# Attention of a hybrid encoder layer: keys loaded for 512 queries, two live bias tables, memory weights transposed on TensorE, queries swapped at another tile, charge 0.84

## The chip, the cores and the metric

The kernel runs on one core of a Trainium2 chip. The metric is the time of one execution on the device in microseconds (us), the median of three runs: 3072.31 us before the change (3069.44 to 3073.78). Five engines work side by side, each in its own order: PE (matmul; PEld is its weight load), DVE (vector), ACT (scalar), POOL (GpSimd), and SP, which here issues every DMA. Each stands until the semaphores of its next instruction are set; what is behind that instruction on the same engine stands too.

## The reference

One layer of an encoder, applied to two sequences, 4096 and 1024 rows of 1024. A projection `w_in` makes the inputs of a Hyena branch (a long convolution), of dilated attention, of attention to 256 memory tokens, and gates; the three branches times their gates go through `w_out`. The change is in the two attentions:

```python
for window, dil in ((128, 1), (512, 4), (2048, 16)):      # 6 heads of 64
    R = window // (2 * dil)                               # always 64 keys to each side
    logits = q @ k.T * E ** -0.5 + bias[bucket((kj - qi) * dil)]   # per residue class of dil
    m = max(logits); p = exp(logits - m); s = sum(p)
    outs.append(p @ v / s); lses.append(m + log(s))
y_att = sum(softmax(lses) * outs)
y_mem = softmax(qm @ km.T * E ** -0.5) @ vm               # 4 heads, 256 tokens
```

## The kernel before

Everything is float32 in value; products take float16 pairs, high and low part, in up to three passes. Stages follow each other: the Hyena projection with the filter beside it; the q, k, v projection with the long convolution beside it; the gate projection with attention beside it (about 1640 to 2576 us); the output.

`weave` mixes two generators: each yields a charge, and the one with the smaller sum goes on. Attention's charges are multiplied by `K_A` = 0.88 while gates run (L140, L1628). This, and `ORDER`, in which a tile's scores, exps, turns and values alternate, set PE's order, which is kept word for word. The other engines and SP are ordered by a scheduler: by the priority at which the code is reached, and by when a model has operands and buffers ready; it can take a later instruction first.

`att_tiles` cuts each residue class of each dilation into groups of up to 256 queries (two tiles of 128). `work_list` mixes these, the second sequence's, and memory groups: 84 groups, 160 tiles, 40 of them memory tiles. For a group, `load_group` issues the transposing loads of the queries `qT` and of the keys `kT` (up to 384 rows: 64 more to each side), and of the values `v`. It is called when the first tile of the group two before is reached (`AHEAD` = 2), and it ends with two DVE copies that put the halves of `qT` in each other's place (`qS`, two buffers, L967 to L971): a score is the product of `qT` and `kT` plus that of `qS` and `kT`.

A tile goes through four steps, each a tile or more behind the last. Scores: PE writes `s`, DVE scales, adds the bias table `tab` and takes the maximum `mx` (L1051). Exps: ACT (L1063). After the first two heads (`XT` = 2), `crossbar` splits these into `hl` on POOL (L1079, L1080), and SP transposes `hl` into `hx` by a DMA (L1082). Turns: the other heads in pairs, four transposes on PE into `tt` (L1094), high part `th` on ACT, low part `tl` on DVE. Values: PE multiplies with `v`, or with `vm` for the memory. `attended` copies the result and the negative maximum into `y`, POOL the maximum (L1155), ACT the rest (L1156), and stores it (`yc`, `ym`). A memory tile has four heads: two by `hx`, two by `tt`. Three bias tables are loaded before the first tile.

Of the kernel before, what the change touches and what calls it, by code (L numbers as in the profile page):

```python
# [12 lines left out]
F32 = mybir.dt.float32  # L13
F32R = mybir.dt.float32r
F16 = mybir.dt.float16
I32 = mybir.dt.int32
AF = mybir.ActivationFunctionType
ALU = mybir.AluOpType
# [4 lines left out]
P = 128  # L23
# [3 lines left out]
H = 6  # L27
# [5 lines left out]
CONFIGS = ((128, 1), (512, 4), (2048, 16))  # L33
C_Q, C_MQ, C_K = 0, 768, 1280
ROW = C_K + 768
# [3 lines left out]
YW = VH + H  # L39
# [97 lines left out]

IDLE_F, K_F, C_FFN = 50000, 2.4, 2000
K_C, IDLE_1, IDLE_2, IDLE_3, IDLE_M = 1.35, (34000, 28000), (9000, 16000), 18000, 40000
K_A, IDLE_A, GATE_IDLE = 0.88, 20000, 0  # L140
LAG_I, WS_BUFS = 6, 6
MT, BATCH0 = 4, 2
MIX, K_Q = 0.1, 1.2
AHEAD = 2
XT, VLAG = 2, 4
ORDER = "etevsteeesvvsetesvsetse"
GP = 6000000
# [31 lines left out]
class Layer:  # L179
# [726 lines left out]
    def att_tiles(self):  # L906

        out = []
        for i, (off, L) in enumerate(self.seqs):
            for cf, (win, dil) in enumerate(CONFIGS):  # L910
                n = L // dil
                if n == 64:
                    for r in range(0, dil, 2):
                        out.append(dict(seq=i, cf=cf, dil=dil, r=r, n=n, pair=True, q0=0, nq=128, k0=0, k1=128))
                    continue
                assert n % 128 == 0
                for r in range(dil):
                    for q0 in range(0, n, 256):
                        q1 = min(n, q0 + 256)
                        out.append(dict(  # L920
                            seq=i, cf=cf, dil=dil, r=r, n=n, pair=False, q0=q0, nq=q1 - q0,
                            k0=max(0, q0 - 64), k1=min(n, q1 + 64),
                        ))
        return out

    def load_group(self, pool, g):
        i, nc = g["seq"], self.nc
        dil, r = g.get("dil", 1), g.get("r", 0)
        rows = self.rows[i].rearrange("(n d) c -> d n c", d=dil)
        vr = self.vrows[i].rearrange("(n d) c -> d n c", d=dil)  # L930
        qT = g["qT"] = pool.tile([P, 6, 256], F16, tag="qT", name="qT", bufs=AHEAD + 1)
        if "mem" in g:
            nc.sync.dma_start_transpose(out=qT[:, 0:4], in_=self.rows[i][g["q0"]:g["q0"] + 256, C_MQ:C_K])
            return
        kT = pool.tile([P, 6, 384], F16, tag="kT", name="kT", bufs=AHEAD + 1)
        nk = g["k1"] - g["k0"]
        v = pool.tile([P, 3, VW], F16, tag="v", name="v", bufs=2)
        if g["pair"]:
            for a in range(2):
                nc.sync.dma_start_transpose(out=kT[:, :, 64 * a:64 * a + 64], in_=rows[r + a, :, C_K:ROW])  # L940
                nc.sync.dma_start_transpose(out=qT[:, :, 64 * a:64 * a + 64], in_=rows[r + a, :, C_Q:C_MQ])
                self.ld(v[64 * a:64 * a + 64, 0, :], vr[r + a])
            g["chunks"] = {0: 0}
        else:
            nc.sync.dma_start_transpose(out=kT[:, :, :nk], in_=rows[r, g["k0"]:g["k1"], C_K:ROW])
            nc.sync.dma_start_transpose(
                out=qT[:, :, :g["nq"]], in_=rows[r, g["q0"]:g["q0"] + g["nq"], C_Q:C_MQ]
            )
            cuts = [g["k0"]] + list(range(g["q0"] + 64, g["k1"], 128))
            ends = cuts[1:] + [g["k1"]]  # L950
            g["chunks"] = {s: j for j, s in enumerate(cuts)}
            full = [j for j, (s, e) in enumerate(zip(cuts, ends)) if e - s == 128]
            part = [j for j, (s, e) in enumerate(zip(cuts, ends)) if e - s != 128]
            if full:
                f0, nf = full[0], len(full)
                assert full == list(range(f0, f0 + nf))
                self.ld(
                    v[:, f0:f0 + nf, :],
                    vr[r, cuts[f0]:cuts[f0] + 128 * nf].rearrange("(j p) c -> p j c", p=P),
                )  # L960
            for j in part:
                k = ends[j] - cuts[j]
                p0 = P - k if j else 0
                nc.gpsimd.memset(v[P - k:P, j, :] if p0 == 0 else v[0:p0, j, :], 0.0)
                self.ld(v[p0:p0 + k, j, :], vr[r, cuts[j]:ends[j]])
        g["kT"], g["v"] = kT, v
        qS = g["qS"] = pool.tile([P, 6, 256], F16, tag="qS", name="qS", bufs=2)  # L967
        for a in range(2):
            nc.vector.tensor_copy(  # L969
                qS[64 * a:64 * a + 64, :, :g["nq"]], qT[64 - 64 * a:P - 64 * a, :, :g["nq"]]  # L970
            )  # L971
# [18 lines left out]
    def attention(self, pool, ps):  # L990
        nc = self.nc
        zero = pool.tile([P, 1], F32, name="zero", bufs=1)
        nc.vector.memset(zero, 0.0)
        groups = self.work_list()
        while groups[0]["seq"] not in self.done:
            yield 500
        self.load_group(pool, groups[0])
        self.load_tables(pool)
        for g in groups[1:AHEAD]:
            self.load_group(pool, g)  # L1000
        yield IDLE_A
        tiles = [(gi, t) for gi, g in enumerate(groups) for t in range(g["nq"] // P)]
        state = {}

        def scores(n):
            gi, t = tiles[n]
            g = groups[gi]
            if t == 0 and gi + AHEAD < len(groups):
                self.load_group(pool, groups[gi + AHEAD])
            mem = "mem" in g  # L1010
            i, q0 = g["seq"], g["q0"] + t * P
            st = state[n] = dict(g=g, q0=q0, mem=mem, H=HM if mem else H)
            if mem:
                W, ls = NMEM, self.lsc[:, 1, 0:1]
                st["chunks"] = [(0, 0), (P, 1)]
                st["v"], st["lo"] = self.vm[i], HM * E1
                units = ((0, 1), (2, 3))
            else:
                ls = self.lsc[:, 0, 0:1]
                if g["pair"]:  # L1020
                    ks, ke, tb, t0 = 0, 128, self.tabp, 0
                    st["chunks"] = [(0, 0)]
                else:
                    ks, ke = max(0, q0 - 64), min(g["n"], q0 + 192)
                    tb, t0 = self.tab[g["cf"]], ks - (q0 - 64)
                    st["chunks"] = [(0, g["chunks"][ks]), (ke - ks - P, g["chunks"][q0 + 64])]
                W, kc = ke - ks, ks - g["k0"]
                st["v"], st["lo"] = g["v"], VH
                units = ((0, 2), (1, 3), (4,), (5,))
            st["W"] = W  # L1030
# [26 lines left out]
        def exps(n):  # L1057
            st = state[n]
            nh, pt, W = st["H"], st["pt"], st["W"]
            nm = st["nm"] = pool.tile([P, H], F32, tag="nm", name="nm", bufs=VLAG + 1)  # L1060
            nc.vector.tensor_scalar_mul(nm[:, :nh], st["mx"][:, :nh], -1.0)  # L1061
            for h in range(nh):
                nc.scalar.activation(out=pt[:, h, :W], in_=pt[:, h, :W], func=AF.Exp, bias=nm[:, h:h + 1])  # L1063
                if h + 1 == XT:
                    crossbar(st)
                yield 0

# [18 lines left out]
        def turns(n):  # L1086
            st = state[n]
            pt, chunks = st["pt"], st["chunks"]
            st["p"] = []
            for pr in range(XT // 2, st["H"] // 2):  # L1090
                tt = ps.tile([P, 2, 2, P], F32, tag="e", name="tt", bufs=2)
                for ci, (w0, vj) in enumerate(chunks):
                    for a in range(2):
                        nc.tensor.transpose(tt[:, a, ci, :], pt[:, 2 * pr + a, w0:w0 + P], self.ident)  # L1094
                th = pool.tile([P, 2, 2, P], F16, tag="th", name="th", bufs=4)
                tl = pool.tile([P, 2, 2, P], F16, tag="tl", name="tl", bufs=4)
                n = len(chunks)
                nc.scalar.activation(out=th[:, :, :n], in_=tt[:, :, :n], func=AF.Copy)  # L1098
                nc.vector.tensor_tensor(out=tl[:, :, :n], in0=tt[:, :, :n], in1=th[:, :, :n], op=ALU.subtract)  # L1099
# [3 lines left out]
        def values(n):  # L1103
# [1 line left out]
            chunks, v, lo = st["chunks"], st["v"], st["lo"]  # L1105
            last = len(chunks) - 1
            yp = ps.tile([P, 512], F32, tag="gf"[n % 2], name="yp", bufs=(1, 3)[n % 2])
            heads = list(range(XT, st["H"])) + list(range(XT))
            st["p"] += [(st["hx"][:, 0, h], st["hx"][:, 1, h]) for h in range(XT)]
            for pr in range(st["H"] // 2):  # L1110
                for a in range(2):
                    h = heads[2 * pr + a]
# [26 lines left out]
    def attended(self, pool, st, yp):  # L1139

        nc = self.nc
        g, q0 = st["g"], st["q0"]
        y = pool.tile([P, YW], F32, tag="y", name="y", bufs=2)
        if st["mem"]:
            sm = pool.tile([P, HM], F32, tag="sm", name="sm", bufs=3)
            yv = yp[:, :HM * E1].rearrange("p (h e) -> p h e", e=E1)
# [413 lines left out]
            t0 = b * B + t * P  # L1560
            self.st(self.out[i][t0:t0 + P, :], xr)

    def load_tables(self, pool):
        nc = self.nc
        self.tab = []
        for cf in range(3):
            t = pool.tile([P, H, 256], F32, name=f"tab{cf}", bufs=1)
            src = self.tab_d[cf]
            self.ld(t, bass.AP(src.tensor, src.offset + P - 1, [[H * 384 - 1, P], [384, H], [1, 256]]))
            self.tab.append(t)  # L1570
        bm = pool.tile([P, P], F32, tag="pt", name="bm", bufs=3)
        self.ld(bm, self.x["bmask"])
        self.tabp = pool.tile([P, H, P], F32, name="tabp", bufs=1)
        nc.gpsimd.tensor_tensor(
            out=self.tabp, in0=self.tab[2][:, :, 64:192], in1=bm.unsqueeze(1).to_broadcast([P, H, P]), op=ALU.add
        )

    def pool(self, name, space=None, side=None):
        kw = {"space": space} if space is not None else {}
# [101 lines left out]
```

## Time and profile before

| | |
|---|---|
| median of three runs | 3072.31 us (3069.44 to 3073.78) |
| the profiled execution | 3067.02 us, its span 3065.2 us |
| PE, DVE, ACT, POOL busy | 91%, 67%, 54%, 41% of the span |
| gate products | 1638.8 to 2574.6 us (first to last start) |
| value products of attention | 1574.4 to 2527.9 us |
| output products | 2576.2 to 3060.5 us |

"Busy" is the share in which the engine has an instruction at work; matmuls overlap, so that the time between two starts, not the length of one, is what PE pays. A wait is put down to what ended it. [...] Times in the rows are us from the span's start, means are ns.

### The profile page before, as it was taken

To read this page: it belongs to the slowest core of one execution; us is meant where nothing else is said; L and a number is where in the kernel's file an instruction comes from. 1 tells how busy PE (TensorE), PEld (TensorE's weight loads), DVE (VectorE), ACT (ScalarE), POOL (GpSimd) and SP (SyncE) were. 2 spreads that over 40 slices of the span, in tenths; PEclk is the share of its full clock that TensorE was granted. 3 is DMA by queue.
4 is the path that set the end of the run, shared out by engine and by line. 5 is a ranking of instruction groups with operands and counts; after the bars stand their busy time and mean duration, and the time that the engine had idled before them with its cause. 6 is when DMAs were issued, how large, how long until landed. Compare 5 with 4: busy or idle time off the path is not lost. (4 is left out here: it accounts for less than half of the span.)

```text
span 3065.2 us, 55390 instructions
## 1 busy us (share of the span) xinstructions
PE 2775.0 (91%) x19620; PEld 1725.3 (56%) x19620; DVE 2052.3 (67%) x5237; ACT 1663.4 (54%) x3149; POOL 1259.7 (41%) x1534
## 2 busy tenths in 40 slices
PE   5998989888959998999999998989899899999999
PEld 2444444333625544544456666666666665778787
DVE  7777888787648882364567666767677665665663
ACT  5666666334738884464366565656566554232321
POOL 2336777232126661142133233333344344555551
PEclk9999999999979999999999999999999999999999
DMA  7554444555559969697499999999998989777762
GB/s 224 175 151 151 155 148 146 155 164 190 208 167 230 246 200 209 214 202 176 110 222 265 216 202 203 225 210 191 210 219 197 202 172 315 250 239 252 236 223 97
DMA packets 761855, 610.38 MB, mean 199 GB/s; under 512 B 514958, under 2 KB 702262, under 8 KB 758122
## 3 DMA queue, kind: packets, MB, share of 16 engines
q1 hardware_dynamic: 761578, 606.84, 75.2%
q8 instruction: 155, 2.54, 0.3%
q14 instruction: 122, 1.00, 0.1%
HBM read 289.08 MB, written 199.92 MB: 160 GB/s over the span
## 5 line engine op out<-in xcount | busy, mean ns | idle before, releaser
L1063 ACT ACTIVATE pt<-pt,nm 128x256 f32<-128x256 f32 (+2 forms) x880 | 350.0, 472 | 182.6 <-DVE nm L1061 171.4
L279 PE MATMUL z<-wA,hA 128*128 128x512 f16 (+1 forms) x960 | 352.5, 367 | 18.1 <-ACT rw L440 14.5
L280 PE MATMUL z<-wA,hA 128*128 128x512 f16 (+1 forms) x960 | 352.7, 367 | 0.0
L281 PE MATMUL z<-wA,hA 128*128 128x512 f16 (+1 forms) x960 | 352.5, 367 | 0.0
L1051 DVE CUSTOM_DVE_ANT_0 pt<-s,tab,lsc 128x256 f32<-128x256 f32 (+1 forms) x672 | 278.9, 449 | 100.9 <-PE s L1047 89.5
L279 PE MATMUL zh<-hB,wh 128*128 128x512 f16 x720 | 280.1, 389 | 25.0 <-ACT zb L877 24.8
L280 PE MATMUL zh<-hB,wh 128*128 128x512 f16 x720 | 279.5, 388 | 1.5 <-DVE hB L384 1.5
L281 PE MATMUL zh<-hB,wh 128*128 128x512 f16 x720 | 279.3, 388 | 0.0
L279 PE MATMUL oo<-wo,mhi 128*128 128x512 f32 x640 | 257.3, 402 | 10.1 <-DVE xr L1557 5.0
L281 PE MATMUL oo<-wo,mlo 128*128 128x512 f32 x640 | 253.8, 397 | 1.3 <-POOL mlo L1536 1.3
L280 PE MATMUL oo<-wo,mhi 128*128 128x512 f32 x640 | 253.7, 396 | 0.0
L1079 POOL CAST hl<-pt 128x256 f16<-128x256 f32 (+1 forms) x212 | 102.8, 499 | 359.4 <-ACT pt L1063 288.3
L279 PE MATMUL zg<-hG,wg 128*128 128x512 f16 x640 | 246.9, 386 | 0.8 <-DVE vr L475 0.7
L280 PE MATMUL zg<-hG,wg 128*128 128x512 f16 x640 | 246.8, 386 | 0.0
L281 PE MATMUL zg<-hG,wg 128*128 128x512 f16 x640 | 246.1, 385 | 0.0
L1099 DVE TENSOR_TENSOR tl<-tt,th 128x512 f16<-128x512 f32 (+1 forms) x280 | 187.8, 673 | 59.9 <-ACT th L1098 58.4
L1098 ACT ACTIVATE th<-tt 128x512 f16<-128x512 f32 (+1 forms) x280 | 159.4, 574 | 102.5 <-PE yp L1120 50.3
L1094 PE MATMUL tt<-ident,pt 128*128 128x128 f32 x1088 | 173.4, 282 | 35.6 <-DVE tl L1099 25.8
L1044 PE MATMUL s<-kT,qT 128*128 128x256 f16 (+2 forms) x720 | 165.6, 261 | 38.2 <-DVE mx L1051 33.9
L1080 POOL TENSOR_TENSOR hl<-pt,hl 128x256 f16<-128x256 f32 (+1 forms) x212 | 190.4, 906 | 6.4
L891 DVE SCALAR_TENSOR_TENSOR u<-zb,cw,u 128x512 f32<-128x512 f32 (+2 forms) x180 | 167.3, 933 | 33.4 <-ACT u L887 29.9
L1094 PEld LDWEIGHTS tt<-ident,pt 128*128 128x128 f32 x1088 | 132.1, 145 | 71.3 <-issue 31.3
(303 smaller groups left out, 7167.7 us busy)
## 6 DMA issues: line engine op xcount, KB each, us to landing
y<-yc SPq DMA_DIRECT2D x120, 198.0 KB, 4.5
yc<-y SPq DMA_DIRECT2D x112, 198.0 KB, 2.8
xt<-in_x SPq DMA_DIRECT2D x40, 512.0 KB, 4.7
hts<-hB SPq DMA_DIRECT2D x10, 2048.0 KB, 6.6
hA<-hts SPq DMA_DIRECT2D x40, 512.0 KB, 5.4
rows<-rw SPq DMA_DIRECT2D x40, 512.0 KB, 4.3
hG<-hts SPq DMA_DIRECT2D x10, 2048.0 KB
gt<-go SPq DMA_DIRECT2D x80, 256.0 KB, 3.3
```

The costliest lines, as they stand in the source:

```text
L279: nc.tensor.matmul(out, pick_l(lh, k), pick_r(rh, k), start=(k == 0), stop=False)
L280: nc.tensor.matmul(out, pick_l(lh, k), pick_r(rl, k), start=False, stop=False)
L281: nc.tensor.matmul(out, pick_l(ll, k), pick_r(rh, k), start=False, stop=(k == n - 1))
L891: nc.vector.scalar_tensor_tensor(out=u[:, :w], in0=zb[:, c0 + d:c1 + d], scalar=cw[:, j, tap:tap + 1], in1=u[:, :w], op0=ALU.mult, op1=ALU ...
L1044: nc.tensor.matmul(s[:, a, :W], g["qT"][:, h, qs], g["kT"][:, h, kc:kc + W], start=True, stop=False,)
L1051: nc.vector.tensor_tensor_reduce(out=pt[:, h, :W], in0=s[:, a, :W], in1=zero.to_broadcast([P, NMEM]) if mem else tb[:, h, t0:t0 + W], scal ...
L1063: nc.scalar.activation(out=pt[:, h, :W], in_=pt[:, h, :W], func=AF.Exp, bias=nm[:, h:h + 1])
L1079: nc.gpsimd.tensor_copy(hl[:, 0, :, c], src)
L1080: nc.gpsimd.tensor_tensor(out=hl[:, 1, :, c], in0=src, in1=hl[:, 0, :, c], op=ALU.subtract)
L1094: nc.tensor.transpose(tt[:, a, ci, :], pt[:, 2 * pr + a, w0:w0 + P], self.ident)
L1098: nc.scalar.activation(out=th[:, :, :n], in_=tt[:, :, :n], func=AF.Copy)
L1099: nc.vector.tensor_tensor(out=tl[:, :, :n], in0=tt[:, :, :n], in1=th[:, :, :n], op=ALU.subtract)
```

## The change

`att_tiles` makes blocks of `KG` = 512 queries; the two groups of a block share one `kT` of up to 640 keys, loaded with the first, and there are three such buffers. The swap of queries is a method of its own, called with the last tile of the group before. Bias tables have two buffers and are loaded when their first group is. Memory tiles send no head through `crossbar` (`st["xt"]` = 0) and turn all four heads on PE. `th` and `tl` have six buffers, `y` three, `K_A` is 0.84.

```diff
-K_A, IDLE_A, GATE_IDLE = 0.88, 20000, 0
+K_A, IDLE_A, GATE_IDLE = 0.84, 20000, 0
-AHEAD = 2
+AHEAD, KG = 2, 512
@@ att_tiles
-                    for q0 in range(0, n, 256):
-                        q1 = min(n, q0 + 256)
-                        out.append(dict(
...
+                    for b0 in range(0, n, KG):
+                        b1 = min(n, b0 + KG)
+                        keys = dict(b0=b0, k0=max(0, b0 - 64), k1=min(n, b1 + 64))
+                        for q0 in range(b0, b1, 256):
...
@@ load_group
-        kT = pool.tile([P, 6, 384], F16, tag="kT", name="kT", bufs=AHEAD + 1)
+        if g["cf"] not in self.tab:
+            self.load_table(pool, g["cf"])
+        if g["pair"] or g["q0"] == g["keys"]["b0"]:
+            kT = pool.tile([P, 6, KG + P], F16, tag="kT", name="kT", bufs=3)
...
-            nc.sync.dma_start_transpose(out=kT[:, :, :nk], in_=rows[r, g["k0"]:g["k1"], C_K:ROW])
+            keys = g["keys"]
+            if g["q0"] == keys["b0"]:
+                keys["kT"] = kT
+                nc.sync.dma_start_transpose(
+                    out=kT[:, :, :keys["k1"] - keys["k0"]], in_=rows[r, keys["k0"]:keys["k1"], C_K:ROW]
+                )
+            kT = keys["kT"]
...
+    def swap_queries(self, pool, g):
+        if "mem" in g:
+            return
+        nc, qT = self.nc, g["qT"]
         qS = g["qS"] = pool.tile([P, 6, 256], F16, tag="qS", name="qS", bufs=2)
         for a in range(2):
             nc.vector.tensor_copy(
...
@@ attention: scores
             if t == 0 and gi + AHEAD < len(groups):
                 self.load_group(pool, groups[gi + AHEAD])
+            if (t + 1) * P == g["nq"] and gi + 1 < len(groups):
+                self.swap_queries(pool, groups[gi + 1])
...
-                st["chunks"] = [(0, 0), (P, 1)]
+                st["chunks"], st["xt"] = [(0, 0), (P, 1)], 0
...
+                st["xt"] = XT
@@ exps, turns, values: XT becomes st["xt"]
-                if h + 1 == XT:
+                if h + 1 == st["xt"]:
                     crossbar(st)
-            for pr in range(XT // 2, st["H"] // 2):
+            for pr in range(st["xt"] // 2, st["H"] // 2):
...
-                th = pool.tile([P, 2, 2, P], F16, tag="th", name="th", bufs=4)
-                tl = pool.tile([P, 2, 2, P], F16, tag="tl", name="tl", bufs=4)
+                th = pool.tile([P, 2, 2, P], F16, tag="th", name="th", bufs=6)
+                tl = pool.tile([P, 2, 2, P], F16, tag="tl", name="tl", bufs=6)
@@ attended
-        y = pool.tile([P, YW], F32, tag="y", name="y", bufs=2)
+        y = pool.tile([P, YW], F32, tag="y", name="y", bufs=3)
@@ load_tables becomes load_table
+    def load_table(self, pool, cf):
+        nc = self.nc
+        t = self.tab[cf] = pool.tile([P, H, 256], F32, tag="tab", name="tab", bufs=2)
...
+        if cf == len(CONFIGS) - 1:
+            bm = pool.tile([P, P], F32, tag="y", name="bm", bufs=3)
...
```

The first place is DVE, in the first dilation, around the swap for the group of queries 2304 to 2559 of the long sequence; the rows on `pt,mx` are one head's scaling, `nm` is the negative maximum that closes a tile. Before:

```order
L1051 ISA pt,mx<-s,tab_14627,lsc 128x256
L1051 ISA mx 128x1
L969 COPY qS<-qT 64x1536 x2
L1051 ISA pt,mx<-s,tab_14627,lsc 128x256
L1051 ISA mx 128x1
L1061 TENSOR_SCALAR nm<-mx 128x6
L1099 TENSOR_TENSOR tl<-tt,th 128x512
```

After:

```order
L1071 ISA pt,mx<-s,tab,lsc 128x256
L1071 ISA mx 128x1
L986 COPY qS<-qT 64x1536 x2
L1081 TENSOR_SCALAR nm<-mx 128x6
L1119 TENSOR_TENSOR tl<-tt,th 128x512
```

The swap stood before the last head of the tile two ahead of its reader; now it stands behind that head, still in front of the tile's `nm`. In all, 20 of the 64 swaps stood 13 heads before their reader and 24 now stand 12 before it.

The second place is SP, around a memory group of the short sequence (`ym_116` is its store, `yc` those of other tiles). Before:

```order
L945 DMA_TRANSPOSE kT<-rows_75 128x6x320
L1082 DMA_TRANSPOSE hx<-hl 128x8x128
L195 DMA gt_1_88<-go 128x512
L192 DMA hG<-hts_3_98 128x8192
L195 DMA ym_116<-y 128x256
L946 DMA_TRANSPOSE qT<-rows_75 128x6x256
L1082 DMA_TRANSPOSE hx<-hl 128x8x128
L195 DMA ym_116<-y 128x256
```

After:

```order
L953 DMA_TRANSPOSE kT<-rows_75 128x6x576
L1102 DMA_TRANSPOSE hx<-hl 128x8x128
L195 DMA ym_116<-y 128x256
L192 DMA hG<-hts_3_98 128x8192
L957 DMA_TRANSPOSE qT<-rows_75 128x6x256
L195 DMA gt_1_88<-go 128x512
L195 DMA ym_116<-y 128x256
```

The `hx` between the load of queries and the second store is gone; the key load is longer, and `qT` keeps its place between the two stores. Over the whole program SP has 1353 rows instead of 1421, with 54 key loads instead of 72. On PE 462 rows instead of 432 follow the last value product.

## Rows read from the trace of the kernel before

**Rows 1.** The page: busy time, share of the span and instructions of each engine.
```profile
PE 2775.0 (91%) x19620; PEld 1725.3 (56%) x19620; DVE 2052.3 (67%) x5237; ACT 1663.4 (54%) x3149; POOL 1259.7 (41%) x1534
```

**Rows 2.** Stretches of attention, then output: length; PE, PEld, DVE, ACT, POOL busy; clock; DMA.
```profile
1640.00:1862.00 222.00, 205.67 (x2276) 147.91 (x2274) 154.23 (x540) 136.61 (x300) 70.52 (x102) 0.96 1.01 224
1862.00:2084.00 222.00, 202.28 (x2267) 145.65 (x2265) 155.80 (x566) 135.48 (x310) 79.89 (x137) 0.97 0.97 206
2084.00:2306.00 222.00, 204.67 (x2326) 147.17 (x2325) 155.64 (x587) 138.81 (x326) 86.26 (x150) 0.98 0.96 207
2306.00:2530.00 224.00, 203.46 (x2362) 144.18 (x2359) 149.11 (x575) 134.69 (x326) 92.32 (x174) 0.98 0.90 192
2576.00:3060.00 484.00, 473.10 (x2112) 380.73 (x2113) 287.65 (x651) 140.43 (x173) 246.21 (x186) 1.00 0.66 222
```

**Rows 3.** The chain that ended last, 1640 to 2530 us, by line.
```profile
by line: DMA qT<-rows 9.0%; PE zg L279 6.9%; PE zg L280 6.9%; PE zg L281 6.8%; PE tt L1094 6.7%; PE s L1044 3.6%; PE s L1047 3.4%; DVE qS L969 3.2%; DVE pt L1051 2.9%; PE yp L1118 2.9%; PE yp L1120 2.8%; PE yp L1119 2.8%; issue 2.7%; DMA hx
```

**Rows 4.** Waits of DVE, 1640 to 2530 us: total, times, longest.
```profile
DVE qS L969 <- DMA qT<-rows: 74.3, 33, 5.4
```

**Rows 5.** Timeline of SP around one late load: start, length, queue, line, operation.
```profile
1884.14 1.44 SPq L1082 DMA_TRANSPOSE hx<-hl  x1
1886.30 1.38 SPq L946 DMA_TRANSPOSE qT<-rows  x1
```

**Rows 6.** Timeline of DVE there; idle time and its releaser in brackets.
```profile
1891.62 1.12 DVE L969 COPY qS<-qT 64x1536 f16<-64x1536 f16 x2 [2.44 <-DMA qT<-rows]
```

**Rows 7.** Timeline of PE there.
```profile
1893.26 0.37 PE L1044 MATMUL s<-kT,qT 128*128 128x256 f16 x1 [2.67 <-DVE mx L1051]
1893.42 0.42 PE L1047 MATMUL s<-kT,qS 128*128 128x256 f16 x1
```

**Rows 8.** Busy time and granted clock just behind that wait.
```profile
1893.00:1896.00 3.00, 2.74 (x11) 1.75 (x11) 2.22 (x10) 2.15 (x6) 1.29 (x3) 0.50 0.65 158
```

**Rows 9.** Issues of hx, 1640 to 2530 us: count, min/median/max ns on SP.
```profile
L1082 SPq DMA_TRANSPOSE hx<-hl x149: 1189/1294/4891, 1645.5 to 2522.5; - x149
```

**Rows 10.** Issues of qT for groups in two tiles, same columns.
```profile
L946 SPq DMA_TRANSPOSE qT<-rows x49: 1321/1532/4377, 1650.7 to 2492.0; - x49
```

**Rows 11.** Issues of kT for groups in two tiles, same columns.
```profile
L945 SPq DMA_TRANSPOSE kT<-rows x48: 1357/2369/8433, 1661.9 to 2489.4; - x48
```

**Rows 12.** Waits of POOL, 1640 to 2530 us.
```profile
POOL y L1155 <- DMA yc<-y: 132.1, 52, 5.8
POOL hl L1079 <- DMA hx<-hl: 63.2, 18, 9.2
```

**Rows 13.** Timeline of PE around one group of four transposes.
```profile
1880.11 0.38 PE L281 MATMUL zg<-hG,wg 128*128 128x512 f16 x1
1880.32 0.60 PE L1094 MATMUL tt<-ident,pt 128*128 128x128 f32 x4
1880.76 0.25 PE L1044 MATMUL s<-kT,qT 128*128 128x192 f16 x1
```

**Rows 14.** Transposes on PE, 1640 to 2530 us: count, busy, mean ns, idle before.
```profile
L1094 PE MATMUL tt<-ident,pt 128*128 128x128 f32 x1013 | 160.9, 281 | 34.7 <-DVE tl L1099 25.8 <-DVE nm L1061 5.7 <-DVE sm L1148 2.5
```

**Rows 15.** Groups of DVE, ACT and POOL, 1575 to 2576 us, same columns.
```profile
L1099 DVE TENSOR_TENSOR tl<-tt,th 128x512 f16<-128x512 f32 x260 | 178.3, 688 | 54.7 <-ACT th L1098 53.3
L1098 ACT ACTIVATE th<-tt 128x512 f16<-128x512 f32 x260 | 151.1, 586 | 94.7 <-PE yp L1120 44.9 <-PE tt L1094 33.5 <-PE yp L1119 15.7
L1051 DVE CUSTOM_DVE_ANT_0 pt<-s,tab,lsc 128x256 f32<-128x256 f32 x342 | 153.0, 480 | 56.3 <-PE s L1047 51.6 <-POOL hl L1079 1.8 <-POOL y L1155 0.9
L1080 POOL TENSOR_TENSOR hl<-pt,hl 128x512 f16<-128x512 f32 x98 | 113.6, 1160 | 5.8
L1079 POOL CAST hl<-pt 128x512 f16<-128x512 f32 x98 | 60.0, 612 | 219.6 <-ACT pt L1063 172.8 <-DMA hx<-hl 43.0 <-issue 3.6
```

**Rows 16.** DMA packets, 1640 to 2530 us.
```profile
DMA packets 408990, 184.39 MB, mean 207 GB/s; under 512 B 361136, under 2 KB 398149, under 8 KB 407716
```

**Rows 17.** Waits of ACT, 1640 to 2530 us.
```profile
ACT y L1156 <- DMA yc<-y: 15.8, 7, 5.6
```

More of the change, by code (lines that the diff above doesn't have):

```diff
@@ L917, in att_tiles @@
                 for r in range(dil):
-                    for q0 in range(0, n, 256):
-                        q1 = min(n, q0 + 256)
-                        out.append(dict(
-                            seq=i, cf=cf, dil=dil, r=r, n=n, pair=False, q0=q0, nq=q1 - q0,
-                            k0=max(0, q0 - 64), k1=min(n, q1 + 64),
-                        ))
+                    for b0 in range(0, n, KG):
+                        b1 = min(n, b0 + KG)
+                        keys = dict(b0=b0, k0=max(0, b0 - 64), k1=min(n, b1 + 64))
+                        for q0 in range(b0, b1, 256):
+                            q1 = min(n, q0 + 256)
+                            out.append(dict(
+                                seq=i, cf=cf, dil=dil, r=r, n=n, pair=False, q0=q0, nq=q1 - q0, keys=keys,
+                                k0=max(0, q0 - 64), k1=min(n, q1 + 64),
+                            ))
         return out
@@ L934, in load_group @@
             return
-        kT = pool.tile([P, 6, 384], F16, tag="kT", name="kT", bufs=AHEAD + 1)
-        nk = g["k1"] - g["k0"]
+        if g["cf"] not in self.tab:
+            self.load_table(pool, g["cf"])
+        if g["pair"] or g["q0"] == g["keys"]["b0"]:
+            kT = pool.tile([P, 6, KG + P], F16, tag="kT", name="kT", bufs=3)
         v = pool.tile([P, 3, VW], F16, tag="v", name="v", bufs=2)
@@ L996, in attention @@
             yield 500
-        self.load_group(pool, groups[0])
-        self.load_tables(pool)
-        for g in groups[1:AHEAD]:
+        self.tab = {}
+        for g in groups[:AHEAD]:
             self.load_group(pool, g)
+        self.swap_queries(pool, groups[0])
         yield IDLE_A
@@ L1026, in scores @@
                     st["chunks"] = [(0, g["chunks"][ks]), (ke - ks - P, g["chunks"][q0 + 64])]
-                W, kc = ke - ks, ks - g["k0"]
+                W, kc = ke - ks, ks - (g["k0"] if g["pair"] else g["keys"]["k0"])
+                st["xt"] = XT
                 st["v"], st["lo"] = g["v"], VH
@@ L1107, in values @@
             yp = ps.tile([P, 512], F32, tag="gf"[n % 2], name="yp", bufs=(1, 3)[n % 2])
-            heads = list(range(XT, st["H"])) + list(range(XT))
-            st["p"] += [(st["hx"][:, 0, h], st["hx"][:, 1, h]) for h in range(XT)]
+            heads = list(range(st["xt"], st["H"])) + list(range(st["xt"]))
+            st["p"] += [(st["hx"][:, 0, h], st["hx"][:, 1, h]) for h in range(st["xt"])]
             for pr in range(st["H"] // 2):
@@ L1561, in output @@
             self.st(self.out[i][t0:t0 + P, :], xr)
-    def load_tables(self, pool):
+    def load_table(self, pool, cf):
         nc = self.nc
[L1565 to L1576, printed above, removed]
+        t = self.tab[cf] = pool.tile([P, H, 256], F32, tag="tab", name="tab", bufs=2)
+        src = self.tab_d[cf]
+        self.ld(t, bass.AP(src.tensor, src.offset + P - 1, [[H * 384 - 1, P], [384, H], [1, 256]]))
+        if cf == len(CONFIGS) - 1:
+            bm = pool.tile([P, P], F32, tag="y", name="bm", bufs=3)
+            self.ld(bm, self.x["bmask"])
+            self.tabp = pool.tile([P, H, P], F32, name="tabp", bufs=1)
+            nc.gpsimd.tensor_tensor(
+                out=self.tabp, in0=t[:, :, 64:192], in1=bm.unsqueeze(1).to_broadcast([P, H, P]), op=ALU.add
+            )
     def pool(self, name, space=None, side=None):
```

## The prediction

> **What bounds the kernel now.** I read the page first, then busy time by stretch, then in the attention stretch the chain, the waits engine by engine, the DMA queues and a few microseconds of timeline. The page [rows 1] says PE 91% busy; the stretches [rows 2] say where the rest is. From 1640 to 2530 us attention tiles are woven with gate products: PE is busy 205.67 + 202.28 + 204.67 + 203.46 = 816.1 of 890 us, so it idles 73.9. The output stage, which the change does not touch, keeps PE at 473 of 484. In attention the DMA engines stand at 0.90 to 1.01, in the output at 0.66 with as many GB/s.
>
> The chain of that stretch [rows 3] has "DMA qT<-rows" first, 9.0% of 890 = 80 us, and "DVE qS" with 3.2%: the load of transposed queries, and the copy that swaps their halves. DVE waits for that load 33 times, 74.3 us [rows 4]. One case [rows 5 to 7]: SP issues hx at 1884.14, then the qT transpose at 1886.30; DVE stands 2.44 us for it until 1891.62; behind the swap stand the last scores' scaling and their maximum; so PE, done with its values, stands 2.67 us before 1893.26. And then it runs at the lower level: granted clock 0.50 over 1893 to 1896 [rows 8]; the next score matmul takes 0.42 us. Clock lost in the stretch: 222 x 0.04 + 222 x 0.03 + 222 x 0.02 + 224 x 0.02 = 24.5 us [rows 2].
>
> Why is the load late? SP is short of time. By medians [rows 9 to 11] three kinds of transposes alone hold it for 149 x 1.29 + 49 x 1.53 + 48 x 2.37 = 381 us of 890, and single issues for up to 4.9, 4.4 and 8.4 us. POOL, which feeds the hx transposes, waits 132.1 us for stores to leave the two y buffers, and 63.2 us for hx to leave hl [rows 12]; an hx that is late on POOL holds up every load behind it on SP.
>
> **The change part by part.** All against the profiled execution, 3067.0 us; the median of the runs is 3072.3, 5.3 higher, and I add the difference at the end.
>
> *Memory weights on TensorE.* 40 memory tiles get one more group of four transposes each. From start to next start a group takes 1880.76 - 1880.32 = 0.44 us [rows 13]: 40 x 0.44 = +17.6 us, all on PE, which issues in order and had no hole there. Upper bound: all transposes with the idle time in front of them, (160.9 + 34.7) / 1013 = 0.193 us each [rows 14], 160 x 0.193 = 31. Below 17.4 is excluded: PE's rows are fixed and this is the full clock. I take 17.6, the row nearest to what is added.
> [...]
>
> DVE gets 40 x 0.688 = 27.5 us and ACT 40 x 0.586 = 23.4 us [rows 15]. DVE is busy 154.23 + 155.80 + 155.64 + 149.11 = 614.8 of 890 (69%, then 72%), ACT 61% then 64% [rows 2]. I take 0; the cover is that PE has the gate products beside each tile. If it is gone, DVE's 0.688 sets the step in place of 0.44: +10. POOL loses 40 x (0.612 + 1.160) = 71 us [rows 15], SP 40 issues.
>
> *Keys for 512 queries.* The key loads fall from 72 to 54 and 18176 to 15872 rows of 1536 bytes, 3.5 MB; with 40 x 262 KB of hx that is 14.0 of 184.4 MB or 8% [rows 16]. Of the packets it is more: most are small (361136 of 408990 under 512 B), and if a transpose moves 128 halves, 256 bytes, at a time, as its shape suggests, 14.0 MB are 55 thousand packets, 13%: an estimate. A longer key transpose can hold SP longer than the 8.4 us seen [rows 11]; they stand some tiles earlier in SP's order than before. 0 to +8, I take +4, together with the table that now loads in mid-stream and the one sum on POOL behind it.
>
> *The swap a tile ahead.* The order says less than the words: in the ordinary case the swap stood before the last head of the tile two ahead of its reader, and now behind it. That is one scaling later, 0.48 us [rows 15], not a tile: qS still has two buffers, and the scheduler takes the first free slot. So this edit alone leaves 1.8 of a mean wait of 74.3 / 33 = 2.25 us.
>
> What shortens the wait is the rest. SP loses 40 x 1.29 = 52 us of hx and 18 key issues; one of four hx no longer stands in front of a load. A third y buffer lets POOL go on instead of waiting 132 us, so the other hx come sooner. With fewer small packets on engines that are 0.90 to 1.01 busy, a load should land some tenths earlier. Together I estimate 1.0 us per wait on top of 0.45: 2.25 falls to 0.8, so 33 x 1.45 = 48 us less on DVE. PE gets back nine tenths of it, by the example even all (2.67 for 2.44): -44. Bounds: 0, and all of PE's idle time, -73.9.
>
> *Clock.* What the shorter waits give back: of 24.5 us I take the same share as of the waits, 44 / 73.9, less a quarter for short drops that stay: -11. Bounds 0 and -24.5.
>
> *Third y, six th and tl.* Directly on PE only little: ACT waits 15.8 us for a store before it may empty the value bank [rows 17]. I take -5, a third of that, bounds 0 and -16.
>
> *Charge 0.84.* A dilated tile is charged 3110, a memory tile 1930 and now 2360: 450400 x 0.88 = 396.4 thousand before, 467600 x 0.84 = 392.8 now. The weave is the same within 1%. In PE's order 462 instead of 432 rows follow the last value product, 15 gate products more, 15 x 0.21 = 3 us [rows 13] that run without attention beside them, and densely either way. 0.
>
> *Sum:* 17.6 + 4 - 44 - 11 - 5 = -38.4. 3067.0 - 38 = 3029, in terms of the median **3034 us**. Late next: scores waiting for DVE's maxima, th waiting for values, and SP's hx.
>
> **The rivals.**
> *The waits stay (slower).* The swap stands where it stood, its load has the same place among the stores in SP's order. For it: the order; against it: the load's lateness comes from what SP does ahead of it, and that is what falls. If less than 22 of the 74.3 us go, PE gets back less than the 17.6 it pays; that is the point from which it decides. With all waits left: 17.6 + 4 - 5 = +17, 3089.
> *It evens out.* A third of the waits goes, 25 us on DVE, 22 on PE; with the clock's share -5, y's -5 and +21.6 that is -10; if DVE's +10 comes too, 0: 3066 to 3078.
> *The waits vanish.* The DMA engines, at 1.01 to 0.90, lose enough that every load lands in time: 17.6 + 4 - 73.9 - 24.5 - 5 = -82, 2990. Against it: all of PE's idle time would have to have one cause, and the chain has many.
> *The transposes cost clock (slower).* If each of the 40 new groups drew one half-clock stretch like the 3 us after 1893 [rows 8], it would lose half of these: 40 x 1.5 = 60 us on top, 3094. Against it: some 250 groups of four stand there already [rows 14], at a mean granted clock of 0.96 to 0.98 [rows 2]. [...]
>
> **How the numbers follow.** Forecast 0.60 (own range 3010 to 3060), even 0.12, waits stay 0.17, waits vanish 0.08, clock 0.03. The runs can tell about 0.2%, 6 us, from no change: faster 0.68, same 0.12, slower 0.20. The bounds add up to -97 and +49; the range 3000 to 3082 leaves out the vanishing waits, the clock case and half of the staying ones, about 0.19.
>
> **What would show it.** In the profile after: four-transpose groups up by 40 at 0.44 us; DVE's wait for qT below 35 us; POOL's wait for y stores near 0; hx issues 120 instead of 160; DMA share in attention at 0.85 to 0.90; PE idle in the stretch 30 to 40 us less beside 17 more busy; clock 0.98 or more. Wrong: a qT wait above 52 us; idle time moving to "tt <- DVE tl" or to scores behind DVE; a clock below 0.96 in tiles of the memory.

## The result, and the profile after

The changed kernel takes 3044.4 us (median of 6 runs), the kernel before 3070.9 us beside it: ratio 0.9918, 95% interval 0.9896 to 0.994. A second series gave 0.9914 (0.989 to 0.9938). The forecast was 3034, a gain of 38; the gain is 26.5. The sum came out near, but two of its terms did not: the shorter wait for the queries did not come, and the larger buffers gave several times what they were priced at.

First the four stretches of attention and the output stage in the changed kernel, columns as in [rows 2]; the clock is the granted clock, the share of its full speed that TensorE had by the trace.

```profile
1640.00:1857.00 217.00, 208.63 (x2363) 152.88 (x2361) 161.34 (x571) 146.68 (x319) 53.27 (x83) 0.98 0.89 212
1857.00:2074.00 217.00, 204.30 (x2338) 150.32 (x2337) 159.29 (x577) 142.74 (x325) 67.89 (x126) 0.98 0.88 200
2074.00:2291.00 217.00, 204.79 (x2334) 148.70 (x2333) 157.46 (x595) 141.47 (x331) 66.12 (x126) 0.98 0.85 193
2291.00:2508.00 217.00, 200.01 (x2336) 144.97 (x2334) 145.15 (x562) 137.07 (x327) 73.54 (x153) 0.99 0.78 182
2557.00:3040.00 483.00, 471.16 (x2115) 379.90 (x2114) 287.05 (x650) 140.35 (x172) 244.73 (x185) 1.00 0.66 222
```

The stretch is 868 us long where it was 890. TensorE is busy 817.7 of it, so it idles 50.3 us; before it was 73.9 [rows 2]. The lost clock falls from 24.5 to 217 x (0.02 + 0.02 + 0.02 + 0.01) = 15.2 us. The DMA share drops by about a tenth, from 0.90 to 1.01 before to 0.78 to 0.89, as the leaner loads and the 40 absent crossbar transposes suggest. Nothing happens in the output stage.

Now the load on which the forecast was built: the chain of the stretch, as in [rows 3], then waits of VectorE, GpSimd and ScalarE as in [rows 4, 12, 17] (DVE, POOL and ACT in the rows).

```profile
by line: DMA qT<-rows 12.2%; PE tt L1114 12.1%; PE zg L279 10.9%; PE zg L280 10.8%; PE zg L281 10.7%; PE s L1064 6.1%; PE s L1067 5.7%; PE yp L1138 4.3%; PE yp L1140 4.2%; PE yp L1139 4.2%; DVE pt L1071 3.3%; PE s L1059 3.0%; DVE tl L1119 2
```

```profile
DVE qS L986 <- DMA qT<-rows: 82.0, 31, 6.4
...
POOL y L1175 <- DMA yc<-y: 114.8, 42, 9.0
POOL y L1175 <- DMA ym<-y: 35.9, 15, 6.5
POOL hl L1099 <- DMA hx<-hl: 24.1, 7, 8.8
...
ACT th L1118 <- PE tt L1114: 97.1, 103, 4.2
```

VectorE's wait for the transposed queries did not shorten: 82.0 us in 31 waits, where 74.3 in 33 stood before [rows 4] and below 35 was forecast. The load's share of the chain went up, 9.0 to 12.2%. GpSimd still waits 114.8 us for stores, not near 0. What did go: ScalarE no longer waits for any store, and at the copy to th it now waits for TensorE's transposes alone. Before, 44.9 + 15.7 us of that idle time had the releaser "PE yp" [rows 15, second row]: the value products, which read th.

The issues of SyncE (SP in the rows), columns as in [rows 9 to 11]; then the DMA packets [rows 16].

```profile
L1102 SPq DMA_TRANSPOSE hx<-hl x111: 1189/1266/4754, 1645.4 to 2501.3; - x111
L957 SPq DMA_TRANSPOSE qT<-rows x49: 1355/1786/5802, 1649.3 to 2469.9; - x49
L953 SPq DMA_TRANSPOSE kT<-rows x33: 1396/1890/5319, 1667.1 to 2464.8; - x33
```

```profile
DMA packets 354378, 170.75 MB, mean 197 GB/s; under 512 B 305938, under 2 KB 343772, under 8 KB 353103
```

SyncE is relieved as forecast, 38 weight and 15 key transposes fewer in the stretch, 13% of the packets gone (54612 of them, with 13.64 MB: 250 bytes on average). So the relief came and the wait stayed. One late load of the changed kernel shows how; first SyncE's timeline, then VectorE's.

```profile
2429.00 0.46 SPq L195 DMA_DIRECT2D yc<-y  x1
2434.50 1.48 SPq L192 DMA_DIRECT2D v<-vrows  x3
2436.08 1.27 SPq L1102 DMA_TRANSPOSE hx<-hl  x1
2437.47 0.51 SPq L195 DMA_DIRECT2D yc<-y  x1
2438.08 1.60 SPq L957 DMA_TRANSPOSE qT<-rows  x1
```

```profile
2444.24 1.12 DVE L986 COPY qS<-qT 64x1536 f16<-64x1536 f16 x2 [3.53 <-DMA qT<-rows]
2445.39 0.42 DVE L1169 TENSOR_TENSOR y<-yp,sm 128x256 f32<-128x256 f32 x1
2445.74 0.68 DVE L1119 TENSOR_TENSOR tl<-tt,th 128x512 f16<-128x512 f32 x1
```

The query transpose follows a weight transpose and a store of results, as most late loads do (26 of 33 have both among the three issues in front). But SyncE stood for neither of these two: it stood 5.04 us, from 2429.46 to 2434.50, in front of a load of values, and then issued everything up to the queries without a break. Values have two buffers in the program, so their load needs the older one free. In the stretch SyncE's plain loads (line 192, most of them of values) wait for TensorE so:

```profile
SPq L192 <- PE yp L1140: 31.7, 11, 5.5
SPq L192 <- PE s L1067: 28.6, 17, 5.2
```

All the late swaps, 33 with two that waited 0.03 us, followed back in the trace: ahead of 12 loads (34 of the 82 us) SyncE had issued for 9 to 45 us without standing 0.3 us, so these are late by its work; before the other 21 it had last stood in front of a load of values (9), a store of gates (6), a weight transpose (5) or a store of results (1). In the timeline above the query transpose left 3.58 us after the load of values for which SyncE had stood 5.04 us, behind the weight transpose and the store in between; and part of what stands in front of such a load waits for TensorE (31.7 and 28.6 us in the rows above), which by way of the swap will wait for the load. The work taken off SyncE turned into standing: its gaps of over 0.2 us add up to 204 us of the stretch, against 134 before. Counted in the order of issue, 54 of the 92 query transposes stand where the eight tiles in front of their reader are not yet stored; before the change 49 do. Behind the swap VectorE now holds a subtraction for tl, where before it held the last scores.

### The profile page after: what moved, and what is told of

The parts are those of the page before. It is cut to its first block, busy times and chain, and to the rows that moved or that the text cites. A ratio compares the mean times of both kernels' runs of the same rounds, so it can differ in the third digit from the quotient of the medians.

```text
span 3042.6 us, 55486 instructions
## 1 busy us (share of the span) xinstructions
PE 2776.7 (91%) x19780; PEld 1737.5 (57%) x19780; DVE 2056.6 (68%) x5277; ACT 1687.8 (55%) x3189; POOL 1186.7 (39%) x1454
## 4 chain that ended last, share of the span: by engine, by line
PE 50%; DVE 12%; DMA 11%; ACT 6%; issue 5%; POOL 3%; SPq 1%; POOLq 0%; DVEq 0%; ACTq 0%
PE oo L279 4%; PE oo L281 4%; PE oo L280 4%; DMA qT<-rows 4%; PE zg L279 4%; PE zg L280 4%; PE zg L281 4%; PE tt L1114 3%; PE z L279 3%; PE z L280 3%; PE z L281 3%; PE s L1064 2%; PE s L1067 2%; DVE pt L1071 1%; DVE u L891 1%
## 5 line engine op out<-in xcount | busy, mean ns | idle before, releaser
L1119 DVE TENSOR_TENSOR tl<-tt,th 128x512 f16<-128x512 f32 (+1 forms) x320 | 214.7, 675 | 61.0 <-ACT th L1118 59.2
L1118 ACT ACTIVATE th<-tt 128x512 f16<-128x512 f32 (+1 forms) x320 | 182.5, 575 | 103.6 <-PE tt L1114 102.5
L1114 PE MATMUL tt<-ident,pt 128*128 128x128 f32 x1248 | 193.2, 276 | 26.1 <-DVE tl L1119 19.0
L1099 POOL CAST hl<-pt 128x256 f16<-128x256 f32 (+1 forms) x172 | 78.1, 471 | 341.0 <-ACT pt L1083 296.5
L891 DVE SCALAR_TENSOR_TENSOR u<-zb,cw,u 128x512 f32<-128x512 f32 (+2 forms) x180 | 164.4, 917 | 32.1 <-ACT u L887 28.6
L1114 PEld LDWEIGHTS tt<-ident,pt 128*128 128x128 f32 x1248 | 149.0, 142 | 59.9 <-issue 17.7
L1067 PE MATMUL s<-kT,qS 128*128 128x256 f16 (+2 forms) x720 | 165.0, 259 | 0.0
```

Source lines behind the costliest of these rows:

```text
L891: nc.vector.scalar_tensor_tensor(out=u[:, :w], in0=zb[:, c0 + d:c1 + d], scalar=cw[:, j, tap:tap + 1], in1=u[:, :w], op0=ALU.mult, op1=ALU ...
L1067: nc.tensor.matmul(s[:, a, :W], g["qS"][:, h, qs], g["kT"][:, h, kc:kc + W], start=False, stop=True,)
L1099: nc.gpsimd.tensor_copy(hl[:, 0, :, c], src)
```

## The experiments

The theories, each naming one part as the source of the gain: S the later swap, M the memory heads off the crossbar, B the larger buffers (Y: those of y; T: those of th and tl), K the longer key loads. Each first run takes one part out of the changed kernel. Ratios are to the kernel before, timed beside them; the changed kernel's is the 0.9914 of its second series. A quotient of two ratios has its interval from both, combined as the root of their squares.

**swap_old.** The swap back in the loading of the group:

```
+        self.swap_queries(pool, g)     # at the end of load_group
...
-        self.swap_queries(pool, groups[0])
...
-            if (t + 1) * P == g["nq"] and gi + 1 < len(groups):
-                self.swap_queries(pool, groups[gi + 1])
```

> The changed kernel with the swap of the queries back where it was (in the loading of a group, two groups ahead); all else as changed. Theory S (the gain of about 20 us in the attention stretch is the later swap, since VectorE then meets the late query transpose with the tile's score work already done): 3058 to 3066 us, VectorE's wait for the query transpose about as long as in the changed kernel (70 to 85 us), but TensorE idle 10 to 20 us longer. Theory M (the memory heads off the crossbar queue): within 4 us of the changed kernel, TensorE idle as there. Theory B (the extra y, th and tl buffers) and theory K (keys for 512 queries): the same, within 4 us.

Measured 0.9932 (0.9918 to 0.9946), 6 us above the changed kernel's 0.9914 (quotient 0.999 to 1.0046): less than the runs resolve, and not the 14 to 22 us of theory S. In all of attention the query wait is 93.8 us (89.8 in the changed kernel) and TensorE idles 64.9 us (61.2).

**mem_xbar.** `st["xt"] = XT` for memory tiles too.

> The changed kernel with the first two memory heads' weights through the crossbar transpose again, as before (40 more such transposes, 40 fewer groups of four on TensorE); all else as changed. Theory M: TensorE does 17.6 us less and yet the time goes up, to 3055 to 3070 us: GpSimd's wait for the weight transposes goes back from 24 to about 60 us and SyncE has some 50 us more work. Theories S, B, K: 3030 to 3045 us, no slower than the changed kernel, since only the TensorE work is taken back.

Measured 0.994 (0.9925 to 0.9955), 8 us above (0.9998 to 1.0055). TensorE does less, and yet the time does not fall. GpSimd's wait for weight transposes is 96.4 us (24.1 in the changed kernel) and the query wait 100.5 over the whole of attention. TensorE is busy 934.8 us in attention against 946.8 in the changed kernel and idles 76 against 61. So what the change adds to TensorE is paid back, perhaps with a little more; that this relief pays it is likely, but only the time and the waits were seen.

**keys256.** `KG = 256`.

> The changed kernel with one key transpose for each 256 queries again (three buffers kept); all else as changed. Theory K (fewer key transposes: SyncE's time for them 48 x 2.37 = 114 us before, 33 x 1.89 = 62 us in the changed kernel): 3052 to 3065 us, SyncE busy some 40 to 50 us longer in the stretch and the wait for the query transpose longer than 82 us. Theories S, M, B: within 4 us; if the long key transpose standing just ahead of a query transpose is what keeps the wait at 82 us, the wait falls below 70 us and the time by up to 10 us.

Measured 0.9935 (0.9914 to 0.9956), 6 us above (0.9989 to 1.0053), though in the stretch SyncE issues 49 key transposes (2.15 us each in the median) in place of 33 (1.89). Not resolved; the query wait does not move, 93.5 us over the whole of attention against 89.8 in the changed kernel.

**bufs_old.** y 3 to 2, th and tl 6 to 4.

> The changed kernel with two y buffers and four th and tl buffers again; all else as changed. Theory B (the waits of ScalarE and GpSimd for the stores of y, 15.8 + 7.4 us on ScalarE before and none in the changed kernel, stood on TensorE's path): 3052 to 3062 us, ScalarE's wait for the stores back at 15 to 25 us. Theories S, M, K: within 4 us of the changed kernel.

Measured 1.0013 (0.9998 to 1.0027): the whole gain is gone, 30 us (quotient 1.0071 to 1.0128). That is more than theory B asked for, and it is the first of the four with a clear answer. The next runs split it.

**after_again, y_old, th_old.** The changed kernel; with `y bufs=2` alone; with `th` and `tl` at `bufs=4` alone.

> The changed kernel itself, unchanged, as the measure for the runs beside it. Both theories below: 0.990 to 0.994 of the kernel before. Were it 0.996 or more, the differences of the first four runs from it would have been partly one of chips.

> The changed kernel with two y buffers again, th and tl kept at six. Taking back all three buffers cost 29 us (ratio 1.0013 against 0.9918). Theory Y (the stores of y held ScalarE and GpSimd): 20 to 29 us above the changed kernel, ScalarE's wait for the stores back near 15 us and GpSimd's near 180 + 60 us. Theory T (the split weights th and tl): at most 6 us above it, though the waits for the stores come back.

> The changed kernel with four th and four tl buffers again, three y kept. Theory T (with the memory heads on TensorE a memory tile fills two of the four th and tl buffers and not one, so ScalarE's copy waits for the value products two tiles back): 20 to 29 us above the changed kernel, ScalarE's wait for the value products at the copy to th at 120 to 150 us, as in the run with all three taken back (86 + 62 us), where the changed kernel shows 97 us for TensorE's transposes alone. Theory Y: at most 6 us above it.

Measured 0.9914 (0.989 to 0.9938), 0.9936 (0.9914 to 0.9959) and 1.0008 (0.9992 to 1.0024). The y buffer is worth 7 us at most likely (0.9989 to 1.0055, not resolved), although GpSimd's waits for y's stores go up from 119.1 + 42.8 to 198.7 + 65.1 us in all of attention: nearly all of that is off the path. The th and tl buffers are worth 29 us (1.0066 to 1.0124). ScalarE's copies to th in th_old, columns as in [rows 15], and TensorE's transposes:

```profile
L1118 ACT ACTIVATE th<-tt 128x512 f16<-128x512 f32 x300 | 175.4, 588 | 153.3 <-PE yp L1140 90.4 <-PE yp L1139 62.3
...
L1114 PE MATMUL tt<-ident,pt 128*128 128x128 f32 x1230 | 193.3, 280 | 59.7 <-DVE tl L1119 46.7 <-DVE nm L1081 13.0
```

The same rows of the changed kernel:

```profile
L1118 ACT ACTIVATE th<-tt 128x512 f16<-128x512 f32 x298 | 173.1, 586 | 97.0 <-PE tt L1114 95.8
...
L1114 PE MATMUL tt<-ident,pt 128*128 128x128 f32 x1224 | 189.1, 276 | 22.2 <-DVE tl L1119 19.0 <-DVE nm L1081 2.3 <-ACT pt L1083 0.4
```

With four buffers ScalarE stands until the value products two tiles back have read them (90.4 and 62.3 of its 153.3 us). From the end of a group's transposes to the end of its th takes 2.11 us in the median, 1.03 with six; to the end of its tl 3.59, and 2.62 with six. By itself this hardly stops TensorE. Followed back in the trace, 41.3 of the 46.7 us that it stands for tl begin with VectorE standing at the swap for a late query load; in the changed kernel 18.1 of 19.0. What the smaller buffers take away is room: when VectorE begins such a stand, the two banks that transposes are written to are both read out in 4 of 40 cases with four buffers and in 12 of 39 with six; both are still full in 6 of the 40, and in none of the 39. So, as far as the traces show, the two causes meet, and the buffers pay mostly where a query load is late. Whether four would still cost 29 us with the queries loaded early, no run tried.

One such place of th_old, on VectorE, then TensorE, then the granted clock:

```profile
1777.12 1.12 DVE L986 COPY qS<-qT 64x1536 f16<-64x1536 f16 x2 [7.04 <-DMA qT<-rows]
1778.28 1.29 DVE L1119 TENSOR_TENSOR tl<-tt,th 128x512 f16<-128x512 f32 x2
```

```profile
1779.11 1.09 PE L1114 MATMUL tt<-ident,pt 128*128 128x128 f32 x4 [7.51 <-DVE tl L1119]
1779.99 0.63 PE L279 MATMUL zg<-hG,wg 128*128 128x512 f16 x1
```

```profile
1779.00:1782.00 3.00, 2.89 (x20) 2.03 (x21) 1.54 (x6) 0.00 (x0) 0.19 (x1) 0.50 0.44 113
```

Here a query wait of 7.04 us holds two subtractions behind the swap, both of them with th already written, TensorE stands 7.51 us for them, and then runs at a granted clock of 0.50, where a group of four transposes is busy for 1.09 us instead of the 0.60 of [rows 13], with 1.00 granted from 1880 to 1881 us.

**b_buf3, b_th.** The kernel before with nothing but three y, six th and six tl; and with six th and tl alone.

> The kernel before with nothing but the larger buffers: three y, six th and six tl. Theory B alone (the buffers are the gain, whatever the rest does): 20 to 28 us below the kernel before, a ratio of 0.991 to 0.994, VectorE's wait for the query transpose still near 74 us. Theory N (the kernel before uses one th and tl pair fewer in a memory tile, so the buffers were needed only to make the memory heads' transposes on TensorE possible): within 6 us of the kernel before, a ratio of 0.998 to 1.002.

> The kernel before with six th and six tl buffers and nothing else (two y). Theory T (the split weights carry the gain): a ratio of 0.993 to 0.997 of the kernel before, most of the 19 us that the larger buffers gave it together, and ScalarE's copy to th no longer waits for value products (65.5 us before). Theory Y (the third y buffer carries it here): 0.998 to 1.002.

Measured 0.994 (0.9919 to 0.996), 18 us below the kernel before, and 0.9952 (0.9935 to 0.9969), 15 us. Theory N falls, theory T stands, and the buffers do not need the memory heads on TensorE to pay. The wait for the value products is gone in b_buf3, and the query wait is not: 97.7 us in all of attention, against 78.5 before. ScalarE's and TensorE's rows as above, then TensorE's largest wait:

```profile
L1098 ACT ACTIVATE th<-tt 128x512 f16<-128x512 f32 x261 | 151.6, 585 | 82.4 <-PE tt L1094 82.1
...
L1094 PE MATMUL tt<-ident,pt 128*128 128x128 f32 x1076 | 169.6, 278 | 21.0 <-DVE tl L1099 11.8 <-DVE nm L1061 3.2 <-ACT pt L1063 2.9
```

```profile
PE s L1044 <- DVE mx L1051: 38.6, 23, 8.4
```

TensorE's stand at tt falls from 34.7 [rows 14] to 21.0; its stand for the scores behind the swap, 33.9 us in all of attention before, is still 38.6.

**q_early, more_buf, both.** What is the query wait worth, then? In q_early, with keys for 256 queries (for room in memory), the query transposes are loaded three groups ahead, into a fourth buffer; more_buf has eight th, eight tl and four y buffers; the third run has both.

```
-AHEAD, KG = 2, 512
+AHEAD, KG = 2, 256
+    def load_queries(self, pool, g):         # the qT transposes, taken out of load_group
+        qT = g["qT"] = pool.tile([P, 6, 256], F16, tag="qT", name="qT", bufs=AHEAD + 2)
...
+                if gi + AHEAD + 1 < len(groups):
+                    self.load_queries(pool, groups[gi + AHEAD + 1])
                 self.load_group(pool, groups[gi + AHEAD])
```

> The changed kernel with keys for 256 queries (ratio 0.9935 in its own run) and the query transposes loaded three groups ahead in place of two, with a fourth buffer. Theory Q (the wait for the query transpose, 82 us in the changed kernel, is still on the path, as the prediction had it): the wait falls below 40 us and the time to a ratio of 0.978 to 0.988. Theory F (the wait falls, but TensorE has other work in it or another wait takes its place): the wait falls below 40 us and the ratio stays within 0.003 of 0.9935. Theory L (the transposes are late for the queue that they stand in, not for their place): the wait stays above 60 us and the ratio too.

> The changed kernel with keys for 256 queries and eight th, eight tl and four y buffers. Theory T at its end (six are enough for two tiles of split weights between their making and the value products): within 0.003 of the 0.9935 of the keys for 256 queries with six, six and three. If more depth still pays: a ratio of 0.986 to 0.990, and GpSimd's wait for the stores of y falls from 115 to under 60 us.

> The query transposes three groups ahead and eight th, eight tl and four y buffers together, with keys for 256 queries. If the two add (theory Q with more depth): 0.972 to 0.984. Theory F: 0.990 to 0.996, no better than the changed kernel's 0.9914.

q_early: **3020.2 us**, 0.9802 (0.9785 to 0.9819), against keys256, from another series, 0.9866 (0.9839 to 0.9893), 41 us less. more_buf: 0.9914 (0.9895 to 0.9932), against keys256 -6 us (0.9951 to 1.0007), not resolved; GpSimd's wait for the larger stores only falls to 81.1 us in the stretch. both: 0.9801 (0.9783 to 0.982), the same as q_early. Theory Q holds; F and L fall, and more depth adds nothing that shows.

All of attention in keys256, then in q_early: for each first the stretch, then VectorE's, GpSimd's and TensorE's waits.

```profile
1551.00:2563.00 1012.00, 947.22 (x10302) 673.06 (x10300) 719.53 (x2586) 648.76 (x1448) 305.53 (x541) 0.98 0.89 208
```

```profile
DVE qS L986 <- DMA qT<-rows: 93.5, 37, 7.6
POOL y L1175 <- DMA yc<-y: 140.7, 43, 11.6
PE s L1064 <- DVE mx L1071: 29.6, 22, 6.3
PE tt L1114 <- DVE tl L1119: 15.5, 12, 2.9
PE yp L1138 <- DMA v<-vrows: 4.5, 1, 4.5
```

```profile
1554.00:2533.00 979.00, 943.25 (x10308) 672.52 (x10306) 720.85 (x2579) 647.37 (x1448) 304.82 (x538) 0.98 0.94 216
```

```profile
DVE qS L998 <- DMA qT<-rows: 24.3, 11, 4.2
POOL y L1191 <- DMA yc<-y: 197.7, 50, 8.8
PE s L1080 <- DVE mx L1087: 5.4, 6, 3.5
PE tt L1130 <- DVE tl L1135: 3.9, 4, 2.8
PE yp L1154 <- DMA v<-vrows: 13.7, 5, 4.8
```

The query wait falls by 69 us, TensorE's idle time from 64.8 to 35.8: both of its waits on VectorE nearly vanish. SyncE issues as many query transposes as before, the DMA engines are busier (0.94 for 0.89) and GpSimd waits longer for its stores; none of that is on the path. What moved is the place: in the order of issue 52 of the 92 loads now stand where the ten tiles in front of their reader are not stored, instead of eight. So they also stand ahead of the value loads of an earlier group; which of the issues passed mattered most was not tried apart. TensorE's wait for the values, 13.7 us, is next.

## Why the prediction was right, and where it was not

*The memory heads' transposes, +17.6.* Right in size: from 1575 us to the end of attention TensorE's transposes are busy 189.1 us in the row above, and 169.3 in the same row of the kernel before (to 2576 us), 19.8 more. None of the 264 whole groups before takes less than 0.435 us from its start to the next, and 40 of these are the 17.4 put down as the floor. But the kernel does not lose by them: without them it is, if anything, 8 us slower (not resolved), with GpSimd and SyncE doing that work again.

*The longer key load and the table, +4.* The sign is not shown: taking the keys back costs 6 us, within the interval of none. The table's new place was not tried alone.

*The swap's wait, -44.* **This is the step that failed:** "What shortens the wait is the rest ... 2.25 falls to 0.8". The wait was put down to how much SyncE has to do; SyncE got less to do, as forecast, and the wait rose to 82.0 us, beyond the mark of 52 set for "wrong". Nor does a load land sooner: 4.4 us after its issue in the median, 4.1 before. Ahead of 21 of the 33 late loads (48 of the 82 us) SyncE had stood shortly before, for what an issue in front of them needed; the other 12 are late behind SyncE's own work, and the change left these at 34 us, 32 before. One group more of lead (q_early) takes most of both away. The price of the wait was too high as well: q_early takes 69 us of it away and gains 41, six tenths, and TensorE's idle time falls by 29; the prediction reckoned 44 and 11 of clock for 48, more than all of it. So the forecast priced a real reserve and credited it to a change that does not touch it. The first sentence of that part had it: the order says less than the words. That the total came out near is luck: the buffers gave what the swap did not.

*Third y, six th and tl, -5.* **The term that was mis-sized:** b_buf3 shows -18 (interval -25 to -12). The prediction looked only at ScalarE's waits for stores [rows 17], which with GpSimd's are worth about 3 to 7 us (b_buf3 against b_th, y_old against after_again; neither resolved). The other wait stood in the rows it quoted: 60.6 us of ScalarE's idle time before th released by value products [rows 15], and behind it 25.8 us of TensorE's by tl [rows 14]. It was listed as "late next" when it was already late. Of those 25.8 us, 22.6 begin with a late query load, so the two terms share the same idle time of TensorE; with 44 of its 73.9 us credited to the swap, little was left for the buffers. In th_old TensorE idles 59.7 us before its transposes, against 22.2 in the changed kernel, though most of these gaps begin at the swap.

*Clock, -11.* Right in size, -9.3 in the stretch, but not from the cause named, since the waits did not get shorter. Which part gives it back is not shown: b_buf3, where TensorE stands as little at its transposes, has a mean granted clock of 0.970 in its runs, as the kernel before beside it, and the changed kernel 0.974.

*The rivals.* The waits stayed, as the first rival had it, and the kernel was faster all the same: its 3089 counted the buffers at 5 us. The clock rival fails: the granted clock of the four stretches, 0.96 to 0.98 before, is 0.98 to 0.99 with 160 more transposes. That each new group would draw a slow stretch was the prediction's supposition; no run shows it. GpSimd's y waits, "near 0", missed; they do not matter.

What stays open: the remaining 8 us between b_buf3 and the changed kernel (quotient 0.9942 to 1.0006) are not assigned to swap, memory heads or keys; each of these, taken back, costs 6 to 8 us, and none of that is resolved. The charge of 0.84 was not tried. The traces also hold about 20 us of difference between executions (the profiled span of the changed kernel was 3042.6 in one series and 3062.9 in the other), so the weights above are from the timed series, and the traces only say where.

## What to carry to other kernels

Where an engine's idle time before a write is ended by the reader of that buffer, buffers may be missing: here 60.6 us of ScalarE's ended so before th, and two more buffers each of th and tl were worth 15 us in b_th. What they are worth depends on the other waits that use up the same room, so look down the releasers of the producers before crediting the bound engine's idle time to one cause. A load that is late on an in-order queue may be late by its place and not by the queue's work, as 21 of the 33 here: ask which issue in front of it stood, and for what. Here taking work off the queue did not shorten the wait, and one group more of lead took away 69 of 93 us.

## What was not expected of the hardware

Removing 13% of the DMA packets in the stretch and a tenth of the DMA engines' busy share (0.78 to 0.89 for 0.90 to 1.01) did not shorten the wait for the query loads, 82.0 us for 74.3; q_early, with "both" the fastest, has a higher share in attention than keys256, 0.94 against 0.89. The median issue of a query transpose took longer on SyncE with fewer transposes about, 1.79 us against 1.53 [rows 10].
